# A transfer-bound GELU-multiply kernel: the first tile loaded in pieces of 1, 3 and 4 rows, the middle tiles computed in steps of five and three rows

## The chip, the cores and the metric

The kernel runs on one core of a Trainium2 chip. The metric is the device time of one execution in microseconds, without the profiler; the span in a profile runs from the first to the last instruction and is 1.8 us shorter. All runs that are compared here are fast, with a granted clock of 1.0. The engines that matter are ACT (ScalarE, here GELU), DVE (VectorE, here the multiply), and the sixteen DMA engines, which SyncE ("SPq") and ACT's queue ("ACTq") feed; in the kernel before, the packets of these two queues take 70.4% and 29.1% of the sixteen engines' time.

## The reference

```python
x = np.random.randn(32, 512, 2048).astype(np.float32)
x1, x2 = x[..., :1024], x[..., 1024:]
out = (0.5 * x1 * (1 + erf(x1 / np.sqrt(2))) * x2).astype(np.float32)
```

Each input element is read once (134.22 MB) and each output element written once (67.11 MB); there is nothing to reuse.

## The kernel before

The 16,384 rows are cut into sixteen tiles of 128 partitions by eight rows. A tile is 8 MiB of input, of which each partition holds eight rows of 8 KB, and 4 MiB of output. Inputs and outputs each have two buffers.

```python
xpool = ctx.enter_context(tc.tile_pool(name="xpool", bufs=2))
opool = ctx.enter_context(tc.tile_pool(name="opool", bufs=2))

def load(i):
    x_tile = xpool.tile([P, R, dim], x.dtype, name="x_tile")
    for rows in (slice(0, 4), slice(4, 8)) if i == 0 else (slice(0, 8),):
        nc.sync.dma_start(out=x_tile[:, rows, :], in_=x_t[i][:, rows, :])
    return x_tile
# ... store(queue, i, o_tile, rows): one dma_start from o_tile ...
ahead = [load(0), load(1)]
for i in range(n_tiles):
    x_tile = ahead.pop(0)
    o_tile = opool.tile([P, R, half], out.dtype, name="o_tile")
    last = i == n_tiles - 1
    pieces = i == 0 or last
    steps = ((0, 2), (2, 4), (4, 8)) if pieces else ((0, 8),)
    for lo, hi in steps:
        rows = slice(lo, hi)
        tc.keep_in_program_order(
            nc.scalar.activation(
                out=o_tile[:, rows, :], in_=x_tile[:, rows, :half], func=GELU
            )
        )
        nc.vector.tensor_mul(
            out=o_tile[:, rows, :],
            in0=o_tile[:, rows, :],
            in1=x_tile[:, rows, half:],
        )
        if pieces and hi % 4 == 0:
            store(nc.sync if last else nc.scalar, i, o_tile, slice(hi - 4, hi))
    if not pieces:
        store(nc.sync if i == n_tiles - 2 else nc.scalar, i, o_tile, slice(0, R))
    if i + 2 < n_tiles:
        ahead.append(load(i + 2))
```

Two loads go out at the start. The load of tile i+2 needs the input buffer of tile i, so it can go out when DVE has finished tile i, at the same moment as that tile's store.

Of the kernel before, what the change touches and what calls it, by code (L numbers as in the profile page):

```python
# [1 line left out]

# [4 lines left out]

GELU = mybir.ActivationFunctionType.Gelu


@with_exitstack
def kernel(
    ctx: ExitStack,
    tc: tile.TileContext,
    x: bass.AP,
    out: bass.AP,
):








    nc = tc.nc
    P = nc.NUM_PARTITIONS

    x_flat = x.flatten_outer_dims()
    out_flat = out.flatten_outer_dims()  # L30
    n_rows, dim = x_flat.shape
    half = dim // 2

    R = 8
    x_t = x_flat.rearrange("(n p r) d -> n p r d", p=P, r=R)
    o_t = out_flat.rearrange("(n p r) d -> n p r d", p=P, r=R)
    n_tiles = x_t.shape[0]

    xpool = ctx.enter_context(tc.tile_pool(name="xpool", bufs=2))
    opool = ctx.enter_context(tc.tile_pool(name="opool", bufs=2))  # L40

    def load(i):
        x_tile = xpool.tile([P, R, dim], x.dtype, name="x_tile")
        for rows in (slice(0, 4), slice(4, 8)) if i == 0 else (slice(0, 8),):
            nc.sync.dma_start(out=x_tile[:, rows, :], in_=x_t[i][:, rows, :])  # L45
        return x_tile

    def store(queue, i, o_tile, rows):
        queue.dma_start(out=o_t[i][:, rows, :], in_=o_tile[:, rows, :])
# [4 lines that stand above are left out]
        o_tile = opool.tile([P, R, half], out.dtype, name="o_tile")  # L54
        last = i == n_tiles - 1
        pieces = i == 0 or last
        steps = ((0, 2), (2, 4), (4, 8)) if pieces else ((0, 8),)
        for lo, hi in steps:
            rows = slice(lo, hi)
            tc.keep_in_program_order(  # L60
# [17 lines that stand above are left out]
# [1 line left out]
_INS = ['x']  # L79
_OUTS = [((32, 512, 1024), 'float32')]  # L80


# [23 lines left out]
```

## Time and profile before

| | before |
|---|---|
| time, median of 6 runs | 471.02 us (470.97 to 471.08) |
| span | 469.2 us |
| DVE / ACT busy | 139.5 / 114.2 us |
| moved | 201.33 MB, 429 GB/s over the span |
| one middle tile, every | 29.03 us |

The timeline of the kernel before shows one tile. The columns are start and length in us, engine, line, operation, result and source, shapes, and in brackets how long the engine had been idle and what ended that. A transfer "lands" when all of it has arrived and whoever waits for it can go on.

```profile
303.85 7.03 ACT L61 ACTIVATE o_tile<-x_tile 128x8192 f32<-128x8192 f32 x1 [21.98 <-DMA out_dram<-o_tile]
310.91 8.69 DVE L65 TENSOR_TENSOR o_tile<-o_tile,x_tile 128x8192 f32<-128x8192 f32 x1 [20.32 <-ACT o_tile L61]
319.63 0.33 SPq L45 DMA_DIRECT2D x_tile<-in_x_dram  x1
319.63 0.36 ACTq L49 DMA_DIRECT2D out_dram<-o_tile  x1
332.88 7.03 ACT L61 ACTIVATE o_tile<-x_tile 128x8192 f32<-128x8192 f32 x1 [22.01 <-DMA out_dram<-o_tile]
```

ACT waits 22 us of every 29 for an output buffer, that is for the store of two tiles earlier. Such a wait can mean two things: that the wait is the price of compute coming late, or that the DMA engines are full and the buffer can't come free sooner. Which of them holds is what the prediction has to decide.

### The profile page before, as it was taken

What the parts mean: (1) busy time and instruction counts of PE and PEld (TensorE: products, weight loads), DVE (VectorE), ACT (ScalarE), POOL (GpSimd) and SP (SyncE); (2) the same over time, 40 slices, a digit from 0 to 9 for tenths busy, and PEclk for the clock granted to TensorE, in tenths of its full rate; (3) what the DMA queues carried; (4) which work ended last, traced back from release to release, by engine and by line L of the source; (5) the groups of instructions that cost most, each with busy time, mean ns of one, the idle gap of its engine ahead of it and who ended that gap; (6) DMA issues with size and microseconds to landing.
All of it is one profiled execution on the core that took longest, in us unless ns stands there. A gap on an engine that the chain in (4) does not pass through costs nothing.

```text
span 469.2 us, 182 instructions
## 1 busy us (share of the span) xinstructions
DVE 139.5 (30%) x20; ACT 114.2 (24%) x21; POOL 0.2 (0%) x4
## 2 busy tenths in 40 slices
DVE  0330332407033070330704307042070520605142
ACT  1320505041050410505005050050501405014060
POOL 0000000000000000000000000000000000000000
DMA  8999999999999999999999999999999999999998
GB/s 358 447 447 447 402 400 495 402 402 447 481 413 402 447 402 492 402 422 427 492 402 402 447 481 413 402 447 430 464 402 425 425 492 402 402 447 492 402 402 358
DMA packets 5040, 201.33 MB, mean 429 GB/s; under 512 B 560, under 2 KB 560, under 8 KB 560
## 3 DMA queue, kind: packets, MB, share of 16 engines
q1 hardware_dynamic: 2880, 142.61, 70.4%
q10 hardware_dynamic: 2160, 58.72, 29.1%
HBM read 134.22 MB, written 67.11 MB: 429 GB/s over the span
## 4 chain that ended last, share of the span: by engine, by line
DMA 72%; DVE 14%; ACT 12%; ACTq 0%; SPq 0%; issue 0%
DMA out_dram<-o_tile 62%; DVE o_tile L65 14%; ACT o_tile L61 12%; DMA x_tile<-in_x_dram 10%; ACTq L101 0%; SPq L45 0%
## 5 line engine op out<-in xcount | busy, mean ns | idle before, releaser
L65 DVE TENSOR_TENSOR o_tile<-o_tile,x_tile 128x8192 f32<-128x8192 f32 (+2 forms) x20 | 139.5, 6985 | 321.2 <-ACT o_tile L61 321.2
L61 ACT ACTIVATE o_tile<-x_tile 128x8192 f32<-128x8192 f32 (+2 forms) x20 | 112.9, 5661 | 341.3 <-DMA out_dram<-o_tile 303.6
L61 ACT ACT_TABLE_LOAD x1 | 1.3, 1283 | 0.7 <-PEq L90 0.7
L90 POOL MEMSET const-bfloat16-1.0<- 128x1 bf16 x1 | 0.1, 102 | 0.0
L90 POOL MEMSET const-uint8-127<- 128x1 uint8 x1 | 0.1, 102 | 0.0
L90 POOL MEMSET const-float32-1.0<- 128x1 f32 x1 | 0.1, 99 | 0.0
L90 POOL MEMSET const-float32-0.0<- 128x1 f32 x1 | 0.1, 98 | 0.2 <-issue 0.2
## 6 DMA issues: line engine op xcount, KB each, us to landing
out_dram<-o_tile ACTq DMA_DIRECT2D x13, 4096.0 KB, 42.2
x_tile<-in_x_dram SPq DMA_DIRECT2D x2, 4096.0 KB, 16.7
out_dram<-o_tile ACTq DMA_DIRECT2D x2, 2048.0 KB, 34.4
out_dram<-o_tile SPq DMA_DIRECT2D x1, 4096.0 KB, 22.7
out_dram<-o_tile SPq DMA_DIRECT2D x2, 2048.0 KB, 7.7
x_tile<-in_x_dram SPq DMA_DIRECT2D x15, 42.1
```

Of the source, the lines that this page charges most:

```text
L61: nc.scalar.activation(out=o_tile[:, rows, :], in_=x_tile[:, rows, :half], func=GELU)
L65: nc.vector.tensor_mul(out=o_tile[:, rows, :], in0=o_tile[:, rows, :], in1=x_tile[:, rows, half:],)
L90: nc = _bacc.Bacc("TRN2", target_bir_lowering=False, num_devices=1)
```

## The change

Its intent: to get compute going earlier in the first tile, and to let DVE start on five rows while ACT still works on the other three, so that a middle tile's load and store go out sooner.

```diff
+    FIRST = (0, 1), (1, 4), (4, 8)
...
-        for rows in (slice(0, 4), slice(4, 8)) if i == 0 else (slice(0, 8),):
-            nc.sync.dma_start(out=x_tile[:, rows, :], in_=x_t[i][:, rows, :])
+        for lo, hi in FIRST if i == 0 else ((0, 8),):
+            nc.sync.dma_start(out=x_tile[:, lo:hi, :], in_=x_t[i][:, lo:hi, :])
...
-        steps = ((0, 2), (2, 4), (4, 8)) if pieces else ((0, 8),)
+        if i == 0:
+            steps = FIRST
+        else:
+            steps = ((0, 2), (2, 4), (4, 8)) if last else ((0, 5), (5, 8))
```

## The prediction

> **What bounds the kernel now.** I read the page first, for the busy shares; then the table of stretches, for whether the DMA engines ever pause; then the chain that ended last and the waits, for what one tile's period is made of; then the timeline, for durations and for the two ends.
>
> The page:
>
> ```profile
> span 469.2 us, 182 instructions
> DVE 139.5 (30%) x20; ACT 114.2 (24%) x21; POOL 0.2 (0%) x4
> ...
> DMA packets 5040, 201.33 MB, mean 429 GB/s; under 512 B 560, under 2 KB 560, under 8 KB 560
> ...
> q1 hardware_dynamic: 2880, 142.61, 70.4%
> q10 hardware_dynamic: 2160, 58.72, 29.1%
> ```
>
> No compute engine works a third of the time. The two DMA queues' packets fill 70.4 + 29.1 = 99.5% of what sixteen DMA engines could have been busy in the span. The table of stretches (stretch and its length, then DVE, ACT and POOL busy, clock, DMA share, GB/s) shows where the rest is:
>
> ```profile
> 0.00:1.70 1.70, 0.00 (x0) 0.97 (x1) 0.20 (x4) 1.00 0.00 0
> 1.70:47.00 45.30, 8.92 (x3) 7.63 (x4) 0.00 (x0) 1.00 1.04 440
> 47.00:62.00 15.00, 7.87 (x1) 7.03 (x1) 0.00 (x0) 1.00 1.01 437
> 62.00:449.00 387.00, 113.83 (x14) 91.38 (x13) 0.00 (x0) 1.00 1.00 431
> 449.00:467.70 18.70, 8.92 (x3) 7.21 (x3) 0.00 (x0) 1.00 0.98 421
> 467.70:469.20 1.50, 0.00 (x0) 0.00 (x0) 0.00 (x0) 1.00 0.00 0
> ```
>
> A packet is counted in the stretch in which it starts, so 1.04 and 0.98 are both a full machine. From 1.70 to 467.70 us there is no pause; nothing moves only in the first 1.70 and the last 1.50 us. A middle tile reads 8 MiB and writes 4 MiB, 12.58 MB. In the chain, successive DVE steps two tiles apart start at 281.89 and 339.95, so 58.06 us for two tiles, 29.03 us each: 12.58 MB / 29.03 us = 433 GB/s. All 201.33 MB at that rate take 464.5 us; with 1.7 and 1.5 us for the ends that is 467.7 of the 469.2 us. The other 1.5 us lie in ramps and small dips.
>
> The chain that ended last looks like something else:
>
> ```profile
> 281.89 8.70 DVE o_tile L65
> 290.60 0.02 issue
> 290.62 42.24 DMA out_dram<-o_tile
> 332.86 0.02 issue
> 332.88 7.04 ACT o_tile L61
> 339.92 0.02 issue
> 339.95 8.71 DVE o_tile L65
> ```
>
> By this list ACT and DVE stand in series with the store: 42.24 + 7.04 + 8.71 + gaps = 58.06 us per two tiles, and the page gives DVE 14% and ACT 12% of the span. **That reading is the trap.** The 42.24 us are not the cost of a 4 MiB store (4.19 MB at 433 GB/s is 9.7 us); they are mostly queueing. When a store is issued, the previous load and store still have 332.86 - 319.65 = 13.2 us to run (the timeline has the issues of the tile before at 319.63), and then its own load and store take 29.03 us: 13.2 + 29.0 = 42.2. If compute gets shorter, the pair is issued earlier and waits longer by just as much.
>
> [...]
>
> **The change part by part.** Durations by shape, from the groups kept apart by shape: ACT 7029 ns (8192 elements a partition), 3608 (4096), 1900 (2048); DVE 8692, 4426, 2288. So ACT is (7029 - 3608)/4096 = 0.835 ns an element plus 187 ns; DVE is (8692 - 4426)/4096 = 1.0415 ns plus 160 ns. A row is 1024 elements. Estimates from these: five rows ACT 4.46, DVE 5.49 us; three rows ACT 2.75, DVE 3.36; one row ACT 1.04, DVE 1.23.
>
> *Middle tiles, steps of five and three rows, x14.* Each adds one ACT and one DVE instruction: 14 x 0.187 = 2.6 us of ACT and 14 x 0.160 = 2.2 us of DVE in all, on engines that idle two thirds of the time. Latency from the ACT start to the end of DVE: before 7.03 + 0.03 + 8.69 = 15.75 us. After: ACT five rows 4.46, DVE five rows 5.49, DVE three rows 3.36 = 13.3 us with gaps (ACT's three rows end at 4.46 + 2.75 = 7.2, well before DVE asks for them at 9.95). That is **2.4 us less per tile**, 14 x 2.4 = 34 us of latency along the compute. The store still goes out whole after the second step and the next load still needs the whole buffer, so both are issued 2.4 us earlier in the cycle. The DMA engines have 13.2 us of queued work then, and would have about 15.6. The period stays 29.03 us. Worth: 0.
>
> *First tile in pieces of 1, 3 and 4 rows.* The first 4 MiB arrives when ACT starts at 12.81, the second at 22.52, so 4 MiB take 9.71 us, one row 2.43. The first row is there at about 12.81 - 3 x 2.43 = 5.5 us, and ACT and DVE do it by 7.8. But no store follows it: a store goes out only when the fourth row is done. Rows 1 to 3 still arrive at 12.8; ACT 2.75 and DVE 3.36 then end at 18.95, against 14.75 + 4.49 = 19.24 before. The first store is 0.3 us earlier, into engines that are loading anyway. The last four rows and their store (30.63 us) don't move, and the second tile's load still lands at 47.05. Added: one DMA with a 0.4 us issue (the first two stand at 0.73 and 1.16) and smaller pieces, 8 and 24 KB a partition. Three loads' issues still end by 2.1 us, far before the first row's 2.43 us of transfer is over, so no gap opens. Worth: 0, perhaps 0.1 us lost for the extra packets.
>
> *The end.* Untouched. From 449 us the engines carry the store of tile 14 (9.7 us, to 458.8) and two half stores of 4.85 us each. The halves are issued at 455.5 and 460.8, when DVE is done (451.02 + 4.49; 456.32 + 4.43), ahead of when the engines come free, 458.8 and 463.6. The last store bounds the end, and its data rate with it.
>
> Sum: 0 + 0 + 0, plus at most 0.1 us.
>
> **The rivals.** (1) *The chain is right*: each tile's 2.4 us comes off the path, every second period loses 4.8 us on its chain, and about seven such round trips save 34 / 2 = 17 us, giving some 454 us. For it: the chain's 26% for ACT and DVE, and 303.6 us of ACT waiting for stores. Against: 201.33 MB in 452 us of span would be 445 GB/s, above the 433 to 437 that any full stretch shows. (2) *Head start*: if the early first row started stores earlier in an idle machine, up to some 5 us could come off the fill. Against: no store follows row one, and DMA share is full from 1.70 us. (3) *Contention or packet cost*: earlier stores and smaller pieces could lower the rate in the fill, or the pairs of loads and stores could fall into a worse order. One per cent of rate would be 4.7 us. Against: the rate is 433 to 437 both in the load-only stretch and in the mixed one. (4) *Tail starved*: were the last load to land later against the stores, the half stores would come late. Their slack is 458.8 - 455.5 = 3.3 and 463.6 - 460.8 = 2.8 us, so shifts of a few tenths cost nothing.
>
> **Range and chances.** The best guess is the time before, 471.0 us. The three runs before lie within 0.11 us; chip to chip and small order effects I allow 0.7 us down and 0.8 up, so 470.3 to 471.8. To be 2% faster needs 461.6 us, whose span would have to move the data at 201.33 MB / (461.6 - 1.8 - 3.2) us = 441 GB/s with no ramp at all (1.8 us is time less span, 3.2 the two ends): 0.01. Slower by 2% needs 9.4 us of new DMA pauses: 0.01. Within 2%: 0.98.
>
> **What would show it.** Right: the span stays at 469.2 within 0.5; a middle tile's store takes 44.6 us to land and not 42.2; ACT idles about 21.8 us per tile and DVE 20.2, and ACT and DVE busy rise to about 117 and 142 us; the first ACT starts near 5.5 us, the first store near 19.0, the second tile's ACT at 47.05 still. DMA share stays 1.00 between 62 and 449 us. Wrong: a period other than 29.03 us per tile; a stretch of low DMA share in the first 60 us; or a gap in the last 20 us between the half stores.

That the middle is at a limit was the estimate from the DMA share of 1.00 at 431 to 433 GB/s; the runs test it. The 0.1 us for the extra packets is a guess that run 1 doesn't resolve (471.21 against 471.10 us, with an interval that includes 1).

## The result and the profile after

The changed kernel took 471.06 us (median of 6 runs, 470.99 to 471.13), the kernel before 471.02 us. The ratio is 1.0001, with a 95% interval of 0.9988 to 1.0013: the same. (Ratios here are the mean time of one kernel's fast runs over that of the other's of the same rounds, so not quite the ratio of the medians quoted.)

The page of the changed kernel:

```profile
span 469.2 us, 213 instructions
DVE 140.6 (30%) x34; ACT 115.7 (25%) x35; POOL 0.2 (0%) x4
...
q1 hardware_dynamic: 3024, 142.61, 70.4%
q10 hardware_dynamic: 2160, 58.72, 29.0%
q14 instruction: 2, 0.02, 0.0%
```

The span is that of before, and so are the two queues' shares but for 0.1% in one. The third queue is new: two packets of kind "instruction" inside the span, of 8 KB and 0.31 us each, which start at 425.8 and 453.6 us. My guess that they fetch the longer program is not shown, nor that they cost anything.

The table of stretches of the changed kernel, for the two ends and what lies between:

```profile
0.00:1.70 1.70, 0.00 (x0) 0.98 (x1) 0.20 (x4) 1.00 0.00 0
1.70:449.00 447.30, 131.66 (x31) 107.46 (x32) 0.00 (x0) 1.00 1.00 434
449.00:467.70 18.70, 8.92 (x3) 7.22 (x3) 0.00 (x0) 1.00 0.92 396
467.70:469.20 1.50, 0.00 (x0) 0.00 (x0) 0.00 (x0) 1.00 0.00 0
```

Again 1.7 us at the start and 1.5 us at the end without transfers, and a DMA share (next to last column) of 1.00 up to 449 us, at 434 GB/s. The last 18.7 us read 0.92 and 396 GB/s, where the kernel before has 0.98 and 421. That isn't the gap at the end which the prediction named as a sign of being wrong: a packet counts where it starts, and by the start and length of each packet in the trace, sixteen are under way from 449 to 466.9 us with no gap (to 467.4 before), and the last one ends at 467.83 us (467.87 before). Most engines finish earlier than before, one as late.

The chain that ended last, for two tiles of the changed kernel:

```profile
229.77 44.64 DMA out_dram<-o_tile
274.41 0.02 issue
274.43 4.48 ACT o_tile L65
278.91 0.02 issue
278.94 8.77 DVE o_tile L69 x2
287.71 0.02 issue
287.73 44.66 DMA out_dram<-o_tile
```

ACT's part on the chain fell from 7.04 to 4.48 us, since DVE starts after five rows. The store grew from 42.24 to 44.64 us, by 2.40, and the sum is the same within 0.1 us: 287.73 - 229.77 = 57.96 us for two tiles, against 58.06 before. A chain piece that grows by what its neighbours lost looks like a queue and not like a cost; the experiments test that.

### The profile page after: what moved, and what is told of

Read it like the earlier page. It is cut to its first block, busy times and chain, and to the rows that moved or that the text cites. A ratio compares the mean times of both kernels' runs of the same rounds, so it can differ in the third digit from the quotient of the medians.

```text
span 469.2 us, 213 instructions
## 1 busy us (share of the span) xinstructions
DVE 140.6 (30%) x34; ACT 115.7 (25%) x35; POOL 0.2 (0%) x4
## 3 DMA queue, kind: packets, MB, share of 16 engines
q1 hardware_dynamic: 3024, 142.61, 70.4%
## 4 chain that ended last, share of the span: by engine, by line
DMA 75%; DVE 14%; ACT 8%; ACTq 0%; SPq 0%; issue 0%
DMA out_dram<-o_tile 66%; DVE o_tile L69 14%; DMA x_tile<-in_x_dram 10%; ACT o_tile L65 8%; ACTq L105 0%; SPq L46 0%; ACTq L65 0%
## 5 line engine op out<-in xcount | busy, mean ns | idle before, releaser
L69 DVE TENSOR_TENSOR o_tile<-o_tile,x_tile 128x3072 f32<-128x3072 f32 (+4 forms) x34 | 140.6, 4171 | 320.6 <-ACT o_tile L65 320.6
L65 ACT ACTIVATE o_tile<-x_tile 128x3072 f32<-128x3072 f32 (+4 forms) x34 | 114.4, 3408 | 340.3 <-DMA out_dram<-o_tile 302.8
## 6 DMA issues: line engine op xcount, KB each, us to landing
out_dram<-o_tile ACTq DMA_DIRECT2D x13, 4096.0 KB, 44.7
```

What stands on the lines that cost most here:

```text
L65: nc.scalar.activation(out=o_tile[:, rows, :], in_=x_tile[:, rows, :half], func=GELU)
L69: nc.vector.tensor_mul(out=o_tile[:, rows, :], in0=o_tile[:, rows, :], in1=x_tile[:, rows, half:],)
```

## The experiments

Twelve kernels ran; all gave the reference's result. Theory A says that the DMA engines are the bound and that earlier compute only lengthens the wait in their queue. Its main rival, C, says that the chain is right: ACT and DVE stand in series with the store. Runs 1 to 4 take the change apart or push it further in its own direction; runs 5 to 7 push the other way, to find where the hidden compute time comes to the surface; run 8 tests the end; runs 9 to 12 follow up on a surprise in run 5.

### 1 and 2. Each part alone

Run 1 has the three pieces of the first tile, the middle tiles whole:

```diff
-            steps = ((0, 2), (2, 4), (4, 8)) if last else ((0, 5), (5, 8))
+            steps = ((0, 2), (2, 4), (4, 8)) if last else ((0, 8),)
```

> Only the first tile's pieces of 1, 3 and 4 rows; the middle tiles in one step as before. Theory A (the DMA engines are full from 1.7 to 467.7 us, so nothing that compute does earlier counts): 471.0 us, within 0.3; a middle store lands 42.2 us after its issue as before; the period stays 29.04 us a tile. Rival B (the two parts act and cancel each other): the pieces alone would be off by more than 0.5 us in one direction, and the middle steps alone by as much in the other. Only ACT and DVE instructions of tile 0 change, so no instruction fetch inside the span.

Measured: 471.21 us (471.06 to 471.24) against 471.10 of before, ratio 1.0003 (0.9991 to 1.0015).

Run 2 has the kernel before with the steps of five and three:

```diff
-        steps = ((0, 2), (2, 4), (4, 8)) if pieces else ((0, 8),)
+        steps = ((0, 2), (2, 4), (4, 8)) if pieces else ((0, 5), (5, 8))
```

> Only the middle tiles in steps of five and three rows; first tile as before. Theory A: 471.0 us, within 0.3, a middle store lands 44.7 us after its issue. Rival C (the chain of waits is the path, ACT and DVE stand in series with the store): about 17 us less, 454. Second-order guess: the period is 29.00 us as in the changed kernel instead of 29.04, for a gain of 0.5 us by tile 13, and two 8 KB instruction fetches on a queue of their own (0.31 us each on one DMA engine) give it back at the end.

Measured: 470.81 us (470.72 to 471.12), ratio 0.9997 (0.9985 to 1.0009); a middle store lands 44.7 us after its issue. Each part is worth nothing by itself, so B, two effects that cancel, falls. The second-order guess about half a microsecond is below what the intervals resolve, and stays open.

### 3. Middle tiles in eight steps of one row

```diff
-            steps = ((0, 2), (2, 4), (4, 8)) if last else ((0, 5), (5, 8))
+            steps = ((0, 2), (2, 4), (4, 8)) if last else tuple((r, r + 1) for r in range(R))
```

> The changed kernel with the middle tiles in eight steps of one row: latency from data to store 8 x 1.23 + 1.06 = 10.9 us instead of 13.3 (changed) or 15.8 (before), the shortest that can be had this way. Theory A: still 471, a middle store lands 47.1 us after its issue; only the added instruction fetches (some 84 more ACT and DVE instructions each than the changed kernel) could cost, 0.3 us each on one DMA engine, so 471.0 to 472.0. Rival C (chain): 7 x 4.9 = 34 us less than before, about 437.

Measured: 471.07 us (median; two of six runs were at 473), ratio 1.0016 (0.9999 to 1.0033). The chain of this kernel:

```profile
227.56 47.61 DMA out_dram<-o_tile
275.18 0.02 issue
275.20 1.06 ACT o_tile L65
276.27 0.02 issue
276.29 9.19 DVE o_tile L69 x8
285.47 0.02 issue
285.50 47.67 DMA out_dram<-o_tile
```

Compute on the chain is down to 1.06 + 9.19 us from 15.75, and the store has taken up all of it but 0.1 us: 47.61 us. C had asked for 437 us and falls. The guess that many more instruction fetches would show was a miss: this profile too has two packets of that kind in the span, though there are some 80 more ACT and 80 more DVE instructions than in the changed kernel.

### 4. A store after each piece of the first tile

```diff
-            if pieces and hi % 4 == 0:
+            if i == 0:
+                store(nc.scalar, i, o_tile, rows)
+            elif last and hi % 4 == 0:
                 store(nc.sync if last else nc.scalar, i, o_tile, slice(hi - 4, hi))
```

> The changed kernel with a store after each piece of tile 0, so that the first store goes out near 7.9 us instead of 19.0. Theory A: 471.0 us within 0.4, because the store only takes time from loads that are queued anyway; the first full load then lands later. Rival D (the early first row fails to help only since no store follows it): several us less, up to 5.

Measured: 471.70 us (471.64 to 473.16), ratio 1.0022 (1.0009 to 1.0034). The first store went out at 8.08 us instead of 19.03, and the kernel got no faster; it lost 0.6 us, a little over what A had allowed. So the first row's early arrival wasn't merely wasted for want of a store behind it (rival D falls). The loads arrive later in return: ACT starts on the last four rows of tile 0 at 25.02 us instead of 22.56, and on tile 1 at 48.57 instead of 47.01. What the 0.6 us are was not taken apart.

### 5, 6 and 7. How much compute the queue hides

In run 5 each middle tile's GELU is computed twice, in run 6 three times, both on the kernel before; run 7 does it three times on the changed kernel. The result is the same, since the repeat overwrites the same rows.

```diff
-            tc.keep_in_program_order(
-                nc.scalar.activation(
-                    out=o_tile[:, rows, :], in_=x_tile[:, rows, :half], func=GELU
-                )
-            )
+            for _ in range(1 if pieces else 2):      # 3 in runs 6 and 7
+                tc.keep_in_program_order(
+                    nc.scalar.activation(
+                        out=o_tile[:, rows, :], in_=x_tile[:, rows, :half], func=GELU
+                    )
+                )
```

> The kernel before, with each middle tile's GELU computed twice (same result), which adds 7.03 us to every middle tile between data and store: 22.8 us instead of 15.8. Theory A (the DMA engines have 13.2 us of queued work when a store is issued): the added time only eats into that, 6.2 us are left, time 471.0 within 0.7, and a middle store lands 35.2 us after its issue instead of 42.2. Rival C (compute in series with the store): 7 x 7.03 = 49 us more, 520.

> The kernel before, with each middle tile's GELU computed three times: 3 x 7.03 + 8.69 = 29.8 us from data to store, more than the 29.03 us that the other tile's pair of transfers lasts. Theory A: now the DMA engines run dry. One tile's cycle is 29.8 us of compute, 29.0 us of transfers and about 2.3 us from issue to first and from last byte to landing (the first 4 MiB load landed 12.05 us after its issue, of which 9.71 are its data), 61.2 us for two tiles instead of 58.07, so 14 x 1.55 = 22 us more: about 492, range 480 to 506. Rival C: 42.24 + 29.8 = 72.0 us for two tiles, about 98 us more, 569.

> The changed kernel (steps of five and three rows, first tile in pieces) with each middle tile's GELU computed three times. From data to store: ACT on all rows 21.7 us, then DVE on three rows 3.36, 25.0 us. Theory A: 25.0 + 29.0 + 2.3 = 56.4 us for two tiles, below the 58.07 that the data need, so the engines stay full: 471.5 within 1.0. The change is then worth about 20 us against the same kernel with whole steps, which shows that the split works and only had nothing to shorten. Rival C: 44.7 + 25.0 = 69.7 us for two tiles, above 550.

| run | middle tile, data to store | expected by A | by C | measured | ratio to before |
|---|---|---|---|---|---|
| 5 twice, whole steps | 22.8 us | 471.0 | 520 | 488.03 | 1.0365 (1.0349 to 1.0380) |
| 6 thrice, whole steps | 29.8 us | 492 | 569 | 514.54 | 1.0954 (1.0889 to 1.1020) |
| 7 thrice, steps of 5 and 3 | 25.0 us | 471.5 | over 550 | 496.92 | 1.0546 (1.0524 to 1.0567) |

C is far off in all three: 98 us of added GELU in run 5 (14 x 7.03) cost 17. But A misses too, by 17 to 25 us, and always in the same direction. My 13.2 us of queued work had been read from a middle round. The **first** round has less. In the trace of the kernel before, tile 1's store and the load of tile 3 go out at 62.86 us, and the pair of transfers before them has landed when ACT starts on tile 2 at 71.62: 8.8 us, not 13.2. In run 5 they go out 7 us later. Its timeline:

```profile
70.06 0.36 ACTq L49 DMA_DIRECT2D out_dram<-o_tile  x1
71.64 14.09 ACT L62 ACTIVATE o_tile<-x_tile 128x8192 f32<-128x8192 f32 x2 [10.34 <-DMA out_dram<-o_tile]
```

Only 1.6 us are left there between the issue and the landing of the work before it, and the engines stumble. By the packet records of this trace no packet of data starts between 70.4 and 71.0 us, and the sixteen load packets that start next, from 71.0 to 72.1, take 2.9 to 4.6 us, where a load packet of this size (64 KB) takes 2.42 in the stream. ACT starts on tile 3 at 104.75 us instead of 100.61, so the first 4 us are lost there. In run 7 the first issue comes at 72.36, after all earlier work has landed (71.48 us in the changed kernel). The rest is stranger. Here is run 5's stretch from 100 to 450 us, long after:

```profile
100.00:450.00 350.00, 96.48 (x12) 168.70 (x24) 0.00 (x0) 1.00 1.00 419
```

The DMA share is 1.00, so no pauses, and yet the rate is 419 GB/s where the kernel before has 432 in the same stretch: the same packets stay longer in the engines. A DMA share of 1.00 went with two rates here, so it did not say that the transfers ran at the higher one.

The packet records say which packets these are. From 100 to 440 us the load packets take 2.55 us on average, against 2.42 in the kernel before, and the store packets 1.21, against 1.22. Over the whole run the load packets' time above 2.42 us comes to 14.9 us an engine (0.5 before), and the engines stand empty for 3.0 us (0.3 before); together that is 17.0 us more, which is about what the span is longer (486.0 against 469.2). The long packets return: fourteen of those that start between 130 and 132 us take 3.2 to 4.6 us.

Run 6, with a DMA share of 0.96 and 395 GB/s between 100 and 450 us, adds what a restart cost in it. Its load of tile 3 and the store beside it were issued at 77.09, some 5 us after everything before had landed (71.64 in run 5, which issued the same transfers before), and the store took 32.49 us to land, against 29.03 us for such a pair in the stream: 3.5 us, where I had counted 2.3. The first sixteen load packets after this pause took 3.8 us on average, and not 2.42, which is 1.4 of the 3.5.

### 8. The last tile whole

The end is the one place with nothing queued behind compute.

```diff
-        steps = ((0, 2), (2, 4), (4, 8)) if pieces else ((0, 8),)
+        steps = ((0, 2), (2, 4), (4, 8)) if i == 0 else ((0, 8),)
...
-            if pieces and hi % 4 == 0:
-                store(nc.sync if last else nc.scalar, i, o_tile, slice(hi - 4, hi))
-        if not pieces:
-            store(nc.sync if i == n_tiles - 2 else nc.scalar, i, o_tile, slice(0, R))
+            if i == 0 and hi % 4 == 0:
+                store(nc.scalar, i, o_tile, slice(hi - 4, hi))
+        if i > 0:
+            store(nc.sync if i >= n_tiles - 2 else nc.scalar, i, o_tile, slice(0, R))
```

> The kernel before, with the last tile computed in one step and stored whole. Theory A: only at the end has compute nothing to hide behind. The last store is issued at 449.07 + 15.75 = 464.8 us, six us after the engines ran dry (458.8), and lands some 12 us later, about 477: 8 to 9 us more, 479.5, range 477 to 482. If the end had slack of its own, it would stay at 471.

Measured: 478.89 us, ratio 1.0167 (1.0150 to 1.0184). The table of stretches of this kernel has the hole:

```profile
449.00:458.50 9.50, 2.42 (x1) 7.03 (x1) 0.00 (x0) 1.00 0.89 386
458.50:465.00 6.50, 6.27 (x1) 0.00 (x0) 0.00 (x0) 1.00 0.00 0
465.00:476.70 11.70, 0.00 (x0) 0.00 (x0) 0.00 (x0) 1.00 0.84 358
```

For 6.5 us DVE works and no transfer starts. Splitting pays here, some 8 us for one tile, and the kernel before had already done it.

### 9 to 12. What made run 5 slow

Four explanations were open for run 5. H: the stumble near 70 us puts the transfers into a slower order, and that persists. G: six microseconds of queued work are too few in every round. F: the added ACT work itself, by its reads and writes, slows the transfers. And the plain view that any added latency costs. Run 9 is run 5 with tile 1 computed once, so that only the first round differs:

```diff
-            for _ in range(1 if pieces else 2):
+            for _ in range(1 if pieces or i == 1 else 2):
```

> GELU twice in the middle tiles, as in the run that took 488 us where 471 had been expected, but once in tile 1. In that run the records of the transfers show that the first queue of work is shorter than later ones: tile 1's store and the third load were issued at 70.06, when the load before had about a microsecond of data left, the engines paused, and load packets stayed slower from then on (415 GB/s, no pauses). Theory H (the pause near 70 us puts the engines out of step and that persists): without it the time is 471 to 474. Rival G (6 us of queued work at the issue is too little in every round, the landing comes 1 to 3 us after the engines need new work): 484 to 488 as before.

Measured: 470.74 us (470.66 to 470.81), against 488.03 of run 5; ratio to before 0.9992 (0.9977 to 1.0007). The same two views for run 9:

```profile
62.88 0.36 ACTq L49 DMA_DIRECT2D out_dram<-o_tile  x1
71.64 14.09 ACT L62 ACTIVATE o_tile<-x_tile 128x8192 f32<-128x8192 f32 x2 [17.51 <-DMA out_dram<-o_tile]
...
123.43 0.36 ACTq L49 DMA_DIRECT2D out_dram<-o_tile  x1
129.58 14.09 ACT L62 ACTIVATE o_tile<-x_tile 128x8192 f32<-128x8192 f32 x2 [14.91 <-DMA out_dram<-o_tile]
```

```profile
100.00:450.00 350.00, 104.31 (x12) 169.95 (x25) 0.00 (x0) 1.00 1.00 432
```

The first issue comes 8.8 us ahead of the landing, the later ones 6.2 us (129.58 - 123.43), and the rate is 432 GB/s. Thirteen tiles with doubled GELU cost nothing; doubling it in tile 1 too costs 17 us. G falls: 6.2 us of queued work are enough here, and run 5's second long burst, at 130 us, follows an issue (127.59) that came just as far ahead of the landing (133.75). So what decides is what went before, as H says. One part of H is not shown: no run doubled the GELU of tile 1 alone, so whether a late first issue stays costly when the later tiles have their 13.2 us is open.

Run 10 puts the same amount of ACT work behind the store of the kernel before:

```diff
+    spool = ctx.enter_context(tc.tile_pool(name="spool", bufs=1))
+    scratch = spool.tile([P, 2, half], out.dtype, name="scratch")
...
+            for r in range(0, R, 2):
+                tc.keep_in_program_order(
+                    nc.scalar.activation(out=scratch, in_=o_tile[:, r : r + 2, :], func=GELU)
+                )
```

> The kernel before with the same amount of extra ACT work as GELU twice (four instructions of 2048 elements a middle tile, 7.6 us, into a scratch tile), but placed behind the store, where ACT waits 22 us anyway. Rival F (extra ACT work itself slows the transfers): 480 or more. Theories G and H (what counts is when the next load and store are issued): 471.0 within 0.7, a middle store still lands 42.2 us after its issue.

Measured: 470.93 us (median; one of four runs at 472.7, which is the profiled one), ratio 1.0005 (0.9988 to 1.0023). F falls.

Run 11 is the changed kernel with GELU twice (the loop of run 5 in the changed kernel):

> The changed kernel with GELU twice in the middle tiles. From data to store: ACT 14.4 us on all rows, then DVE on three rows 3.36, 17.8 us instead of 22.8 with whole steps. The first such store goes out near 65 us, 5 us before the data of the load before end. Theory (issue early enough and nothing is lost): 471.5 within 1.5, so the steps of five and three rows are worth about 16 us against the 488 of whole steps with the same compute. If the split gave nothing at all even there: 488.

Measured: 471.21 us, ratio 1.0002 (0.9987 to 1.0017). The first middle tile's store goes out at 65.20 us, 6.6 us before ACT can start on tile 2. With this heavier compute, the steps of five and three rows decide between 488.03 and 471.21 us. The change does what it intends; the kernel before only had nothing for it to shorten.

Run 12 repeats GELU on four of the eight rows, 3.6 us more per middle tile:

```diff
+            if not pieces:
+                tc.keep_in_program_order(
+                    nc.scalar.activation(
+                        out=o_tile[:, 4:8, :], in_=x_tile[:, 4:8, :half], func=GELU
+                    )
+                )
```

> The kernel before with GELU computed again on four of eight rows of the middle tiles, 3.6 us more from data to store: 19.4 us. First store of a middle tile at about 66.5 us, some 3.4 us before the data of the load before end; later ones with about 9 us of queued work. Theory (the margin ends where the issue comes within about 3 us of the end of the queued data): 471 to 475. A chain in series would give 7 x 3.6 = 25 us more, 496.

Measured: 471.00 us, ratio 0.9999 (0.9982 to 1.0016). Its first store goes out at 66.49 us, and the work before has landed when ACT starts on tile 2 at 71.54: 5.0 us. So a first issue that came 5.0 us ahead of that landing cost nothing, and one that came 1.6 us ahead went with 488.03 us (run 5). That any added latency costs, the plain view, falls with this run and run 9.

What stays open is how the transfers of run 5 stay slower for 400 us after the stumble. The traces show that they do and that it is the load packets that take longer, not why. No version beat both kernels clearly: the lowest medians, 470.74 (run 9) and 470.81 (run 2), have intervals that include 1.

## Why the prediction was right

**The bound.** The step that decided was to divide a tile's bytes by its period and find 433 GB/s, at a DMA share of 1.00 and with no pause from 1.70 to 467.70 us. That about 433 is a limit for these transfers is shown by the runs, in which shorter compute did not raise it; which part of the path sets it, no run tests. The changed kernel moves at 434 between 1.7 and 449 us, and cutting compute on the chain by a third in run 3 did not move it (432 GB/s from 62 to 449 us, against 431 before). One reading was loose: the prediction has 433 to 437 GB/s in any full stretch, but its own table shows 440 up to 47 us and 431 from 62 to 449, since packets count where they start; and the stretch to 47 us is not load-only (its second queue moved 2.10 MB). So its case against rival 1, which needed 445, was thinner than it reads; run 3 makes up for that.

**The chain as a trap.** The store's landing was forecast at 44.6 us; it is 44.64. In the forecast, ACT would idle 21.8 us a tile; the waits of the changed kernel give 302.8 us over 14, 21.6. The same account works with the sign turned round, in run 9: a landing of 35.2 us had been expected of 7 us more compute, and 35.13 came.

**The first tile.** The first ACT starts at 5.56 us (5.5 forecast), the first store goes out at 19.03 (near 19.0), and tile 1's ACT starts at 47.01 (47.05). Run 1 shows the pieces to be worth nothing alone; run 4 that an earlier store would not have helped.

**The extra instructions.** DVE and ACT were to rise to about 142 and 117 us; they rose to 140.6 and 115.7, about half of the rise. The two steps of a middle tile, which follow each other directly, overlap a little: DVE's take 5.49 and 3.35 us by their own durations and 8.76 together, ACT's 4.47 and 2.75 and together 7.12. It made no difference.

**The end.** The slack of the half stores was put at 3.3 and 2.8 us. In the changed kernel ACT started on the last tile 0.4 us later (449.48 for 449.07), and the last store still landed in time for the same span. A period other than 29.03 us was named as a sign of being wrong; it is 28.98 (57.96 / 2), which no time shows. Run 8 shows what the slack protects.

**What was too simple.** The 13.2 us of queued work hold for the middle rounds only. For this change, which makes issues earlier, it didn't matter. For a change that makes them later, it would have: the first round's 8.8 us, of which somewhere between 1.6 (run 5) and 5.0 us (run 12) have to stay, are the real margin, and my own expectations of runs 5 to 7 failed on it.

## What to carry to other kernels

Before shortening compute, divide bytes by period. Here that gave 433 GB/s, about the most that this kernel's transfers kept up (434 over 447 us in the changed kernel); the chain in which compute stood in series with a store was a queue, and the store grew by what compute lost. Splitting a tile paid where nothing is queued behind it (the last tile, 8 us) or where compute nearly filled the margin (488 to 471 us with doubled GELU). Take that margin from the tightest round, here the first after the fill, and not from the steady state.
